# A decoder layer on one core: x loaded a second time, transposed, in place of the first norm's transposes

## The chip, the cores and the metric

The kernel runs on one core of a Trainium2 chip. The metric is the device time of one execution in microseconds (us). An execution uses five engines that run their own instruction queues in order: TensorE (PE in the profile, with its weight loads as PEld), VectorE (DVE), ScalarE (ACT), GpSimd (POOL) and SyncE (SP, which here issues nearly all DMAs). Semaphores order the queues against each other.

## The reference

One layer of a decoder trunk with 256 positions of width 1024, all in float32. Cut to what matters here:

```python
h = rmsnorm(x, ln1_g)                       # x: (256, 1024)
z = h @ w_in                                # 1024 x 2824: pool, mLSTM q/k/v/gates, attention q/k/v
po = pool_mixer(z[pool])                    # windowed means, then 64 x 64 products
hm = mlstm(silu(conv4(z[mq])), silu(conv4(z[mk])), z[v], gates i and f)
ao = attention(rmsnorm(z[aq]), rmsnorm(z[ak]), z[av])
x = x + concat(po, rmsnorm(hm) * sigmoid(z[o]), ao) @ w_out
h2 = rmsnorm(x, ln2_g)
u = conv3(h2 @ w_up)                        # 1024 x 5632
x = x + (silu(u[:2816]) * u[2816:]) @ w_down
```

`rmsnorm(x, g)` is `x * rsqrt(mean(x * x) + eps) * g`. The factor `rsqrt(...)` belongs to a position, the gain `g` to a channel.

## The kernel before

**Products in two parts.** A float32 operand is split into a rounded part "hi" (ACT, `split_hi`, L183) and the rest "lo" (DVE, `split_lo`, L190), and a product is made of three fast matmuls, hi x hi, hi x lo and lo x hi (`product_cols`, `product_rows`, L311 to L322). Where one side is used only once, a plain float32 matmul of the unsplit operands stands in their place (`of_rows`, L446, for the pairs in `FULL`).

**Units.** The weights come in units of 128 partitions by 2048 columns (1 MB), in the order in which PE uses them: unit 0 "of" (output gate and forget gate of the mLSTM, 2080 columns), unit 1 "vi" (values and input gate, 2080), unit 2 pool, 3 mq, 4 mk, 5 akA, 6 aqA and so on, then w_out, w_up and w_down. Four raw buffers (`RAW_BUFS`) hold units as loaded. `load(u)` makes SP issue the load of a unit; `split_lo`, at the last part of unit u, calls `load(u + 4)`, so that load waits in SP's queue until the buffer's readers are done.

**The first norm.** PE needs x with channels on the partitions. x's rows, with the gains beside the first of them, are loaded as `xg` (L216, L217, L220). `first_transpose` (L348) transposes 8 blocks of 128x128 for each half t of the positions, `first_evict` multiplies by the gain on the way out of PSUM (DVE L353, ACT L357), and `first_hi`, `first_lo` (L360, L363) split the result. The norm's factor of a position is not needed for the products: it is put in when they are evicted. `norm_square` (L262) sums the squares of x's rows on ACT, `first_sum` (L371) makes means of them, `guess` (L501, L502) and `newton` (L507 to L509) the factors, and `factors_t` (L385) with `factors` (L389) spread them over the partitions as `rb` for products that have channels on the partitions.

**From the first units on.** ACT evicts of and vi with the factors (`evict_of` L452, L453; `evict_vi` L457, L458). The gate columns of both, for both halves, are transposed by PE (`pg`, L577). From these ACT makes logarithms (`ga`, L582 to L584) and DVE a minimum and two scans (`gm`, `gs`, L589 to L597; L596 copies the running maxima `mr`). The maxima are spread over all partitions by two DMAs that ACT issues: `bm` (L603) writes them to a scratch in DRAM, `br` (L606) reads them back, as soon as `bm` has landed. POOL then masks them (`bs`, L611). DVE evicts pool (`plz`, L781) for a chain of window sums on POOL, and mq and mk (`cz`, L463); ACT scales by the last convolution tap (`cy`, L468), DVE adds the three other taps (`ct`, L476). When all four are done, ACT loads the sigmoid table, makes the sigmoids (`sig`, L485, L488) and loads the old table again (L234). The mLSTM scores (`mS`, L639) follow. akA and aqA are evicted by ACT with squares (`hq`, L515).

**The order of the work** is written out by hand. Every step is a "piece" with a place, a number, from the table `PLACE` or from the default at its `put`. Pieces are emitted in the order of their places, and each engine runs its instructions in that order. PE's products of the bulk, four pieces to a unit, have the whole numbers from 4 on as places: 4 to 7 vi, 8 to 11 pool, 12 to 15 mq, 16 to 19 mk. For example `("hi", 3, 1)`, ACT's split of unit 3's second half, has place 8.84, `bm` 10.076, `br` 10.366, and `("hi", 4, 0)` 9.145.

Before all this PE runs eight matmuls on constants (`keep_warm`, L330), and two more after the first transposes.

Of the kernel before, what the change touches and what calls it, by code (L numbers as in the profile page):

```python
# [9 lines left out]
F32 = mybir.dt.float32  # L10
# [6 lines left out]
P = 128  # L17
# [13 lines left out]
FULL = {(0, q) for q in range(4)} | {(1, 0), (1, 1)}  # L31
# [6 lines left out]
    "n1g": 4.69, "n1n": 4.747, "rbt": 7.327, "rb": 9.568, ("of", 0): 5.309, ("of", 1): 6.265, ("vi", 0): 7.109,  # L38
    ("vi", 1): 7.926, "setup": 5.815, "gain": 16.054, "pg": 7.939, "ga": 8.677, "gm": 9.662, "gs": 9.816,
    "gc": 10.938, "gco": 12.594, "gce": 14.852, ("ply", 0): 41.083, ("plh", 0): 41.762, ("pll", 0): 42,  # L40
    ("ply", 1): 40.544, ("plh", 1): 40.785, ("pll", 1): 41.559, ("plz", 0): 10.494, ("plz", 1): 15.089,
# [54 lines left out]
}  # L96
SPLITS = (4.6, 5.6, 7.6, 9.6, 10.6, 11.6, 12.6, 13.6, 14.6, 16.6)


IN_UNITS = ["of", "vi", "pool", "mq", "mk", "akA", "aqA", "akB", "aqB", "avA", "avB"]  # L100
OUT_K = [0, 2, 4, 6]
N_IN = len(IN_UNITS)
N_OUT = len(OUT_K)
N_DOWN = D_FF // 256
U_OUT = N_IN
U_UP = U_OUT + N_OUT
U_DOWN = U_UP + NPAIR
# [21 lines left out]
def kernel(  # L129
    ctx: ExitStack,  # L130
    tc: tile.TileContext,
    x: bass.AP,
    w: bass.AP,
    wg: bass.AP,
    first: bass.AP,
    params: bass.AP,
    consts: bass.AP,
    out: bass.AP,
):
    nc = tc.nc  # L140

# [43 lines left out]
    def split_lo(u, part, parts):  # L185
# [5 lines left out]
        if part == parts - 1:  # L191
            load(u + RAW_BUFS)
# [1037 lines left out]
```

## Time and profile before

| | us |
|---|---|
| median of 3 runs | 311.16 |
| lowest, highest | 311.11, 312.52 |
| the profiled execution's span | 311.5 |
| PE busy in it | 303.7 (97%) |
| DVE busy | 227.8 (73%) |
| ACT busy | 184.8 (59%) |
| POOL busy | 16.7 (5%) |
| loads and stores of all DMA queues | 54.21 MB, mean 174 GB/s |

The profile is of one execution; its times run from the span's start, which is the first instruction. A row of the instruction views begins with start and duration in us, the engine, the line of the kernel, the operation, and the tiles that it writes and reads ("out<-in"). A bracket tells how long the engine had been idle before and what released it. "SPq" and "ACTq" are those engines' queues of DMA issues. A row of the chain of waits has start, duration and the work on the path that ended last. A row of the waits has the waiting engine and line, whom it waited for, the sum in us, how often, and the longest. In the table of windows each engine's busy time is followed by the granted clock of PE, the DMA engines' busy share and GB/s. The engines' busy shares by themselves decide nothing: PE is busy for 97% of the span, but what it waits for in the remaining time is set by the other queues.

### The profile page before, as it was taken

The page shows a single profiled execution, that of the slowest core. Times are in us where ns is not written, and L with a number is a line of the kernel's source. Part 1 is how long each engine was busy: PE and PEld are TensorE (multiplying, and loading weights), DVE is VectorE, ACT ScalarE, POOL GpSimd, SP SyncE. Part 2 cuts the span into 40 slices and gives each one's busy share as a digit, 9 for nine tenths or more (in the row PEclk, how much of TensorE's full clock was granted, in tenths as well). Part 3 has the DMA queues.
Part 4 walks back from the last instruction along what each step waited for, and adds up shares of the span by engine and source line. Part 5 has one row for each costly group of instructions (what it writes and reads, how often), then busy time and mean ns, then how long its engine had stood idle before and what let it go on. Part 6 is the DMA issues. An engine that isn't in the chain of part 4 may idle for free.

```text
span 311.5 us, 5437 instructions
## 1 busy us (share of the span) xinstructions
PE 303.7 (97%) x2146; PEld 279.0 (90%) x2146; DVE 227.8 (73%) x441; ACT 184.8 (59%) x361; POOL 16.7 (5%) x30
## 2 busy tenths in 40 slices
PE   6999999899999999999999999999999999999995
PEld 3799999899987789999999999999999988888883
DVE  0499899999868657689988788788788786534111
ACT  5398649976888426957575565665664594324000
POOL 1001980000000000000000000000000000000000
PEclk9799999999999999999999999999999999999999
DMA  7985925333704670243564553654544649700003
GB/s 226 424 341 184 347 86 206 128 137 135 263 9 155 252 267 4 97 175 97 185 260 137 179 225 138 203 204 151 214 179 154 239 155 393 276 0 0 0 11 126
DMA packets 8681, 54.21 MB, mean 174 GB/s; under 512 B 964, under 2 KB 1232, under 8 KB 2640
## 3 DMA queue, kind: packets, MB, share of 16 engines
q1 hardware_dynamic: 8352, 52.95, 46.6%
q10 hardware_dynamic: 304, 0.92, 0.9%
q8 instruction: 17, 0.28, 0.3%
q14 instruction: 8, 0.07, 0.1%
HBM read 52.81 MB, written 1.05 MB: 173 GB/s over the span
## 4 chain that ended last, share of the span: by engine, by line
PE 91%; ACT 4%; DVE 3%; issue 1%; DVEq 0%; ACTq 0%
PE dn L824 20%; PE up L313 12%; PE up L311 12%; PE up L312 12%; PE wo L824 7%; PE of L446 2%; DVE mqT L476 2%; PE upr L320 1%; PE upr L322 1%; PE upr L321 1%; PE warm L330 1%; DVE lo L190 1%; PE akB L320 1%; PE n1pt L348 1%; PE pool L311 1%
## 5 line engine op out<-in xcount | busy, mean ns | idle before, releaser
L190 DVE TENSOR_TENSOR lo<-raw,hi 128x1024 fp32r<-128x1024 f32 (+2 forms) x102 | 115.2, 1153 | 18.5 <-ACT hi L183 18.3
L183 ACT ACTIVATE hi<-raw 128x1024 fp32r<-128x1024 f32 (+2 forms) x102 | 98.3, 991 | 28.2 <-PE dn L824 18.6
L311 PE MATMUL up<-h_hi,hi 128*128 128x256 f32 x320 | 90.4, 282 | 0.0
L313 PE MATMUL up<-h_hi,lo 128*128 128x256 f32 x320 | 90.3, 282 | 0.0
L312 PE MATMUL up<-h_lo,hi 128*128 128x256 f32 x320 | 90.3, 282 | 0.0
L313 PEld LDWEIGHTS up<-h_hi,lo 128*128 128x128 f32 x320 | 60.8, 190 | 0.0
L311 PEld LDWEIGHTS up<-h_hi,hi 128*128 128x128 f32 x320 | 60.8, 190 | 0.0
L312 PEld LDWEIGHTS up<-h_lo,hi 128*128 128x128 f32 x320 | 60.8, 190 | 0.0
L1085 DVE SCALAR_TENSOR_TENSOR fy<-up,par,fy 128x255 f32<-128x255 f32 x88 | 41.8, 480 | 15.4 <-ACT fy L1082 13.9
L1082 ACT ACTIVATE fy<-up,par 128x256 f32<-128x256 f32 x44 | 20.1, 466 | 32.4 <-PE up L313 32.4
L824 PE MATMUL dn<-hi,a_hi 128*128 128x512 f32 x88 | 28.1, 392 | 0.0
L824 PE MATMUL dn<-lo,a_hi 128*128 128x512 f32 x88 | 28.1, 392 | 0.0
L824 PE MATMUL dn<-hi,a_lo 128*128 128x512 f32 x88 | 28.1, 392 | 0.0
L824 PEld LDWEIGHTS dn<-hi,a_lo 128*128 128x128 f32 x88 | 16.5, 188 | 3.8
L824 PEld LDWEIGHTS dn<-lo,a_hi 128*128 128x128 f32 x88 | 16.5, 188 | 3.8
L824 PEld LDWEIGHTS dn<-hi,a_hi 128*128 128x128 f32 x88 | 16.5, 188 | 3.7
L238 ACT ACTIVATE a_hi<-fy 128x256 fp32r<-128x256 f32 x22 | 9.2, 418 | 11.8 <-DVE fy L1091 11.8
L1133 DVE TENSOR_TENSOR xg<-dn,xg 128x512 f32<-128x512 f32 (+1 forms) x5 | 2.7, 580 | 16.7 <-PE dn L824 16.7
L824 PE MATMUL wo<-hi,mix_hi 128*128 128x512 f32 x32 | 11.3, 412 | 0.0
L824 PE MATMUL wo<-lo,mix_hi 128*128 128x512 f32 x32 | 10.6, 393 | 0.0
L824 PE MATMUL wo<-hi,mix_lo 128*128 128x512 f32 x32 | 10.6, 393 | 0.0
L1090 ACT ACTIVATE fy<-fy 128x256 f32<-128x256 f32 x22 | 9.0, 408 | 2.2 <-DVE fy L1085 2.2
(287 smaller groups left out, 535.1 us busy)
## 6 DMA issues: line engine op xcount, KB each, us to landing
raw<-in_w SPq DMA_DIRECT2D x46, 1024.0 KB, 4.8
raw<-in_wg SPq DMA_DIRECT2D x2, 520.0 KB, 7.0
raw<-in_wg SPq DMA_DIRECT2D x1, 1040.0 KB
mb<-far ACTq DMA_DIRECT2D x1, 768.0 KB, 7.0
out_y<-xg SPq DMA_DIRECT2D x3, 256.0 KB, 2.1
xg<-in_x SPq DMA_DIRECT2D x1, 512.0 KB, 8.2
par<-in_params SPq DMA_DIRECT2D x1, 337.0 KB, 12.3
xg<-in_first SPq DMA_DIRECT2D x1, 260.0 KB, 2.8
```

What stands on the lines that cost most here:

```text
L183: nc.scalar.activation(hi_t[u][:, s], raw_t[u][:, s], AF.Copy)
L190: nc.vector.tensor_sub(lo_t[u][:, s], raw_t[u][:, s], hi_t[u][:, s].bitcast(F32))
L238: nc.scalar.activation(hi, src, AF.Copy)
L311: nc.tensor.matmul(dst, a, h_hi[:, k, :], start=k == 0, stop=False)
L312: nc.tensor.matmul(dst, a, h_lo[:, k, :], start=False, stop=False)
L313: nc.tensor.matmul(dst, b, h_hi[:, k, :], start=False, stop=k == KT - 1)
L320: nc.tensor.matmul(dst, h_hi[:, k, ts_], hw[:, k, :], start=k == 0, stop=False)
L446: nc.tensor.matmul(ps_t["of", t], h_f[t][:, k, :], w0[:, k, :], start=k == 0, stop=k == KT - 1)
L824: nc.tensor.matmul(acc[t, c], a, b[:, k, o:o + n], start=st and i == 0, stop=sp and i == 2)
L1082: nc.scalar.activation(y, ps[j], AF.Copy, scale=pcol(c0 + 4 * NPAIR))
L1085: nc.vector.scalar_tensor_tensor(y[:, d:], ps[j][:, :S - d], pcol(c0 + 2 * NPAIR * tap), y[:, d:], op0=ALU.mult, op1=ALU.add)
L1090: nc.scalar.activation(y_t[i, 0], y_t[i, 0], AF.Silu)
```

## The change

x is given to the kernel twice: as rows, as before, and transposed (`_xt`: channels on the partitions, the gains in the first 8 columns). The transposed copy, 2056 columns, takes the first raw buffer.

- **Loads.** SP issues, in turn, a quarter of x transposed and a quarter of unit 0, four times; then unit 1's first half, x's rows 0 to 127, unit 1's second half, x's rows 128 to 255; then unit 2, the parameters and the constants. Unit 3 is no longer issued at the start: x transposed holds its buffer, and `split_lo` issues units 3 and 4 together after the last part of unit 0.
- **First norm.** The 16 transposes, their evictions and the two matmuls on constants behind them are gone. For channel blocks of quarters 0 and 1 DVE multiplies by the gain (`first_full`, two instructions of 128x256 a quarter) and PE uses plain float32 products for both halves of the positions; for quarters 2 and 3 `first_hi` and `first_lo` take the gain in themselves, two instructions of 128x256 each, and the product is of three parts. So 8 pairs of channel block and position half are plain products where 12 were.
- **Order.** The first norm's pieces get new places. Both halves of unit 1's rows use its first half of the channels before its second. The sums of squares stand later, just before the guess. Other places that differ:

| piece | before | after |
|---|---|---|
| of, evicted by ACT, t = 0 and 1 | 5.309, 6.265 | 6.2, 6.6 |
| hi of unit 2 | 5.291, 1.571 | 6.4, 6.8 |
| hi of unit 3 | 7.269, 8.84 | 9.95, 10.5 |
| lo of unit 3 | 8.954, 10.243 | 10.1, 10.7 |
| hi of unit 4 | 9.145, 8.886 | 11.75, 12.0 |
| hi of unit 5, first half | 10.09 | 13.6 |
| hi of unit 6, first half | 11.144 | 15.3 |
| lo of units 4 and 5, first halves | 11.57, 13.369 | 11.9, 13.8 |

All others from `rb` (9.568), `bm` and `br` on stay as they were.

```diff
-FULL = {(0, q) for q in range(4)} | {(1, 0), (1, 1)}
+FULL = (0, 1)
...
         if part == parts - 1:
-            load(u + RAW_BUFS)
+            load(u + RAW_BUFS - (u == 0))
+            if u == 0:
+                load(RAW_BUFS)
...
-    nc.sync.dma_start(xg[:, :KT + 512], first[:, :KT + 512])
-    nc.sync.dma_start(xg[:, KT + 512:KT + D], first[:, KT + 512:])
-    load_first(0)
-    load_first(1)
-    nc.sync.dma_start(xs[:, 1], x)
-    load(1)
+    for q in range(4):
+        c = slice(KT * (q > 0) + 2 * S * q, KT + 2 * S * (q + 1))
+        nc.sync.dma_start(x_t[:, c], xt[:, c])
+        load_part(0, q, 4)
+    for t in range(NT):
+        load_part(1, t, 2)
+        nc.sync.dma_start(xs[:, t], x[t * P:(t + 1) * P])
     load(2)
     nc.sync.dma_start(par, params)
-    load(3)
     nc.sync.dma_start(con, consts)
...
+    def first_full(q):
+        for k in (2 * q, 2 * q + 1):
+            nc.vector.tensor_scalar(h_f[:, k, :], xk[:, k, :], g1[:, k:k + 1], None, op0=ALU.mult)
+
+    def first_hi(q):
+        if q in FULL:
+            nc.scalar.activation(h_hi[:, pair(q), :], h_f[:, pair(q), :], AF.Copy)
         else:
+            for k in (2 * q, 2 * q + 1):
+                nc.scalar.activation(h_hi[:, k, :], xk[:, k, :], AF.Copy, scale=g1[:, k:k + 1])
+
+    def first_lo(q):
+        if q in FULL:
+            nc.vector.tensor_sub(h_lo[:, pair(q), :], h_f[:, pair(q), :], h_hi[:, pair(q), :].bitcast(F32))
+        else:
+            for k in (2 * q, 2 * q + 1):
+                nc.vector.scalar_tensor_tensor(h_lo[:, k, :], xk[:, k, :], g1[:, k:k + 1],
+                                               h_hi[:, k, :].bitcast(F32), op0=ALU.mult, op1=ALU.subtract)
...
+    for q in range(4):
+        put(("hi", 1, q), do(split_hi, 1, q, 4), at=(-0.5, 0, 4.4, 4.5)[q])
+        put(("lo", 1, q), do(split_lo, 1, q, 4), ("hi", 1, q), at=(0.5, 1, 4.45, 4.55)[q])
     for t in range(NT):
+        put(("n2", t), do(norm_square, t, 0, 1, "n1", sq1[:, t * D:(t + 1) * D]), at=(4.3, 4.6)[t])
+        put(("sum", t), do(first_sum, t), ("n2", t), at=4.65)
...
-    put("n1g", lambda: guess("n1", n1v[0], [P, NT], "n1"), ("sum", 0), ("sum", 1), at=4.1)
-    put("n1n", do(first_factors), "n1g")
+    put("n1g", lambda: guess("n1", n1v[0], [P, NT], "n1"), ("sum", 0), ("sum", 1), at=4.7)
+    put("n1n", do(first_factors), "n1g", at=4.8)
```

More of the change, by code (lines that the diff above doesn't have):

```diff
@@ L37 @@
 PLACE = {
[L38 to L41, printed above, removed]
[54 rows of a table removed]
+    "rbt": 7.327, "rb": 9.568, ("of", 0): 6.2, ("of", 1): 6.6, ("vi", 0): 7.109, ("vi", 1): 7.926, "setup":
+    5.815, "gain": 16.054, "pg": 7.939, "ga": 8.677, "gm": 9.662, "gs": 9.816, "gc": 10.938, "gco": 12.594, "gce":
+    14.852, ("ply", 0): 41.083, ("plh", 0): 41.762, ("pll", 0): 42, ("ply", 1): 40.544, ("plh", 1): 40.785, ("pll",
[10 rows of a table added]
+    "akA", 1): 23.75, ("hs", "akA", 1): 24.457, ("qe", "aqA", 0): 25.713, ("hq", "aqA", 0): 26.819, ("hs", "aqA",
[11 rows of a table added]
+    "aqB", 0): 34.278, ("qe", "aqB", 1): 35.11, ("hq", "aqB", 1): 37.937, ("hs", "aqB", 1): 37.95, ("hm", "akB"):
[22 rows of a table added]
 }
@@ L134 @@
     wg: bass.AP,
-    first: bass.AP,
+    xt: bass.AP,
     params: bass.AP,
@@ L197, in split @@
             split_lo(u, part, parts)
-    xg = cpool.tile([P, KT + NT * D], F32, name="xg")
-    g1 = xg[:, :KT]
-    xs = xg[:, KT:].rearrange("p (t d) -> p t d", d=D)
+    xs = cpool.tile([P, NT, D], F32, name="xs")
     ident = cpool.tile([P, P], F32, name="ident")
@@ L208, with load_part @@
     nc.gpsimd.affine_select(ident, ones, [[-1, P]], ALU.is_equal, 0.0, base=0, channel_multiplier=1)
+    x_t = wpool.tile([P, UMAX], F32, tag="raw", name="x_t", bufs=RAW_BUFS)
+    g1 = x_t[:, :KT]
+    xk = x_t[:, KT:KT + KT * S].rearrange("p (k c) -> p k c", c=S)
     raw_t[0] = wpool.tile([P, UMAX], F32, tag="raw", name="raw0", bufs=RAW_BUFS)
-    def load_first(c):
-        n = UMAX // 2
-        nc.sync.dma_start(raw_t[0][:, c * n:(c + 1) * n], wg[0][:, c * n:(c + 1) * n])
-    nc.sync.dma_start(xg[:, :KT + 512], first[:, :KT + 512])
-    nc.sync.dma_start(xg[:, KT + 512:KT + D], first[:, KT + 512:])
-    load_first(0)
-    load_first(1)
-    nc.sync.dma_start(xs[:, 1], x)
-    load(1)
+    raw_t[1] = wpool.tile([P, UMAX], F32, tag="raw", name="raw1", bufs=RAW_BUFS)
+    def load_part(u, c, parts):
+        n = UMAX // parts
+        nc.sync.dma_start(raw_t[u][:, c * n:(c + 1) * n], wg[u][:, c * n:(c + 1) * n])
+    for q in range(4):
[5 more added lines that the diff above has]
+        nc.sync.dma_start(xs[:, t], x[t * P:(t + 1) * P])
     load(2)
     nc.sync.dma_start(par, params)
-    load(3)
     nc.sync.dma_start(con, consts)
@@ L337, with pair @@
     table("natural_log_exp_and_others")
-    h_f, r_t, pt1 = {}, {}, {}
+    r_t = {}
     h_fb = wpool.tile([P, UMAX], F32, tag="hi", name="h_f", bufs=HL_BUFS)
+    h_f = h_fb[:, :KT * S].rearrange("p (k c) -> p k c", c=S)
     sq1 = wpool.tile([P, UMAX], F32, tag="lo", name="sq1", bufs=HL_BUFS)
     rb = cpool.tile([P, S], F32, name="rb")
-    HALVES = (slice(0, 4), slice(4, 8))
-    def first_transpose(t):
-        pt1[t] = [aux([P, 4, P], f"n1pt{t}_{b}") for b in range(2)]
-        h_f[t] = h_fb[:, t * D:(t + 1) * D].rearrange("p (k c) -> p k c", c=P)
-        for k in range(KT):
-            nc.tensor.transpose(pt1[t][k // 4][:, k % 4, :], xs[:, t, k * P:(k + 1) * P], ident)
-    def first_evict(t, b, i=0):
-        if (t, b) != (0, 1):
-            ks = HALVES[b]
-            nc.vector.tensor_tensor(h_f[t][:, ks, :], pt1[t][b], g1[:, ks].unsqueeze(2).to_broadcast([P, 4, P]),
-                                    op=ALU.mult)
-        else:
-            for k in range(4 + 2 * i, 6 + 2 * i):
-                nc.scalar.activation(h_f[t][:, k, :], pt1[t][1][:, k - 4, :], AF.Copy, scale=g1[:, k:k + 1])
-    def first_hi(t, b):
-        nc.scalar.activation(h_hi[:, HALVES[b], t * P:(t + 1) * P], h_f[t][:, HALVES[b], :], AF.Copy)
-    def first_lo(t, b):
-        nc.vector.tensor_sub(h_lo[:, HALVES[b], t * P:(t + 1) * P], h_f[t][:, HALVES[b], :],
-                             h_hi[:, HALVES[b], t * P:(t + 1) * P].bitcast(F32))
+    def pair(q):
+        return slice(2 * q, 2 * q + 2)
+    def first_full(q):
[4 more added lines that the diff above has]
+            nc.scalar.activation(h_hi[:, pair(q), :], h_f[:, pair(q), :], AF.Copy)
+        else:
+            for k in (2 * q, 2 * q + 1):
[7 more added lines that the diff above has]
+                                               h_hi[:, k, :].bitcast(F32), op0=ALU.mult, op1=ALU.subtract)
     n1v = []
@@ L442, in of_rows @@
         ks = range(2 * q, 2 * q + 2)
-        if (t, q) in FULL:
+        if q in FULL:
             w0 = operand(raw_t, 0)
             for k in ks:
-                nc.tensor.matmul(ps_t["of", t], h_f[t][:, k, :], w0[:, k, :], start=k == 0, stop=k == KT - 1)
+                nc.tensor.matmul(ps_t["of", t], h_f[:, k, t * P:(t + 1) * P], w0[:, k, :], start=k == 0,
+                                 stop=k == KT - 1)
         else:
@@ L837, in do @@
         return lambda: f(*a)
-    for t in range(NT):
-        put(("T", t), do(first_transpose, t), at=(-9, -8)[t])
-        if t == 0:
-            put(("W", t), do(keep_warm, 2), ("T", t))
-        put(("n2", t), do(norm_square, t, 0, 1, "n1", sq1[:, t * D:(t + 1) * D]), at=(-8.9, 3.8)[t])
-        put(("sum", t), do(first_sum, t), ("n2", t), at=3.9)
-        put(("e", t, 0), do(first_evict, t, 0), ("T", t))
-        for i in range(2 - t):
-            put(("e", t, 1, i), do(first_evict, t, 1, i), ("T", t))
-        for i in range(2):
-            put(("h", t, i), do(first_hi, t, i), *([("e", t, 1, n) for n in range(2 - t)] if i else [("e", t, 0)]))
-            put(("l", t, i), do(first_lo, t, i), ("h", t, i))
@@ L853 @@
-    for u in range(2):
-        for q in range(4):
-            if u == 0 and {(0, q), (1, q)} <= FULL:
-                continue
-            put(("hi", u, q), do(split_hi, u, q, 4), *((("hi", u, q - 1),) if ("hi", u, q - 1) in pieces else ()), at=-7 + 5 * u + q)
-            put(("lo", u, q), do(split_lo, u, q, 4), ("hi", u, q), *((("lo", u, q - 1),) if ("lo", u, q - 1) in pieces else ()))
-    for t in range(NT):
-        for q in range(4):
-            made = [k for k in pieces if k[:3] == ("e", t, q // 2)] if (t, q) in FULL else (("l", t, q // 2), ("lo", 0, q))
-            put(("of", t, q), do(of_rows, t, q), *made, *((("of", t, q - 1),) if q else ()),
-                at=(-4, -2)[t] + q * 0.7)
+    for q in range(4):
+        at = 2 * q - 9
+        if q in FULL:
+            put(("f", q), do(first_full, q), at=at)
+        else:
+            put(("hi", 0, q), do(split_hi, 0, q, 4), at=at + 0.8)
+            put(("lo", 0, q), do(split_lo, 0, q, 4), ("hi", 0, q), at=at + 1.2)
+        put(("h", q), do(first_hi, q), *([("f", q)] if q in FULL else []), at=at + 0.5)
+        put(("l", q), do(first_lo, q), ("h", q), at=at + 1)
+        for t in range(NT):
+            put(("of", t, q), do(of_rows, t, q), *([("f", q)] if q in FULL else [("l", q), ("lo", 0, q)]),
+                *([("of", t, q - 1)] if q else []), at=at + 1.5 + 0.2 * t)
@@ L864 @@
+    for q in range(4):
+        put(("hi", 1, q), do(split_hi, 1, q, 4), at=(-0.5, 0, 4.4, 4.5)[q])
+        put(("lo", 1, q), do(split_lo, 1, q, 4), ("hi", 1, q), at=(0.5, 1, 4.45, 4.55)[q])
+    for t in range(NT):
+        put(("n2", t), do(norm_square, t, 0, 1, "n1", sq1[:, t * D:(t + 1) * D]), at=(4.3, 4.6)[t])
+        put(("sum", t), do(first_sum, t), ("n2", t), at=4.65)
     n = 4
@@ L866 @@
     for name in IN_UNITS[1:]:
-        for j in range(2):
-            for half in range(2):
-                f = bulk_rows if name[:2] in ("vi", "av", "aq", "ak") else bulk_cols
-                put(("b", n), do(f, name, j, half), at=n)
-                done[name, j] = ("b", n)
-                n += 1
+        f = bulk_rows if name[:2] in ("vi", "av", "aq", "ak") else bulk_cols
+        order = [(0, 0), (0, 1), (1, 0), (1, 1)]
+        for j, half in sorted(order, key=lambda o: o[::-1]) if name == "vi" else order:
+            put(("b", n), do(f, name, j, half), at=n)
+            done[name, j] = ("b", n)
+            n += 1
     OUT_ORDER = ((0, 0), (0, 1), (1, 0), (1, 1), (2, 0), (3, 0))
@@ L998 @@
         if n < 8:
-            need(("b", n), ("lo", 1, 1 + 2 * (n % 2)), ("l", n // 6, n % 2))
+            half = n // 6
+            need(("b", n), ("lo", 1, 1 + 2 * half), ("l", 1 + 2 * half))
         elif n < 44:
-            need(("b", n), ("lo", n // 4, n % 2), ("l", 0, 1), ("l", 1, 1))
+            need(("b", n), ("lo", n // 4, n % 2), ("l", 3))
         elif n < 56:
@@ L1196, in _params, with _xt @@
     return p
-def _first(v):
-    return np.ascontiguousarray(np.concatenate([v["ln1_g"][0].reshape(KT, P).T, v["x"][0][:P]], 1))
+def _xt(v):
+    xt = v["x"][0].T.reshape(KT, P, S).transpose(1, 0, 2).reshape(P, KT * S)
+    return np.ascontiguousarray(np.concatenate([v["ln1_g"][0].reshape(KT, P).T, xt], 1))
 def _consts():
@@ L1219 @@
     arrays = {
-        "in_x": np.ascontiguousarray(v["x"][0][P:]), "in_w": w, "in_wg": wg, "in_first": _first(v), "in_params": _params(v),
+        "in_x": v["x"][0], "in_w": w, "in_wg": wg, "in_xt": _xt(v), "in_params": _params(v),
         "in_consts": _consts(),
```

97 rows, old and new, of the table PLACE are left out of this document.

## The prediction

> **What bounds the kernel now.** I read the page, then who TensorE (PE) waited for, then the chain of waits in order of time, then the first 60 us of each queue.
>
> ```profile
> span 311.5 us, 5437 instructions
> ```
> ```profile
> PE of L446 <- DVE h_lo L363: 2.2, 1, 2.2
> ...
> PE akB L320 <- ACT aqAsq L515: 0.8, 1, 0.8
> PE mS L639 <- DVE mkT L492: 0.2, 1, 0.2
> ```
>
> PE is the busy engine, and after the first norm it waits only twice, 1.0 us together: at the first mLSTM scores (mS) and at the first akB product. This looks as if whatever starts PE earlier is gained in full. The chain of waits says what those two waits hang on:
>
> ```profile
> 4.41 1.45 PE n1pt L348 x8
> ...
> 8.49 4.56 PE of L446 x12
> 13.05 0.87 PE n1pt L348 x8
> 13.93 2.63 PE of L446 x12
> ...
> 18.00 0.13 PE vi L320
> ...
> 23.73 0.44 PE n1r L385 x4
> 24.17 0.44 PE pg L577 x4
> ...
> 36.63 0.42 DVE mqz L463
> ...
> 45.46 0.34 DVE mkz L463
> ...
> 46.25 0.46 ACT akAsq L515
> ...
> 56.83 0.39 PE akB L320
> ```
>
> Up to 36.6 us the chain is PE's. Then it is VectorE's (DVE) for nine microseconds, from the second mq eviction to the second mk eviction, then ScalarE's (ACT) through two table loads until akB gets its PSUM buffer at 56.83. PE is not idle meanwhile, but it has only the 0.8 us in hand. So two things must come early for the end to come early: PE's queue, and DVE's arrival at the second mq eviction. If PE comes early and DVE does not, PE simply waits longer at mS and akB.
>
> **The loads.** The change adds a second copy of x, so I count bytes first.
>
> ```profile
> 0.81 0.38 SPq L216 DMA_DIRECT2D xg<-in_first  x1
> ...
> 2.66 0.43 SPq L220 DMA_DIRECT2D xg<-in_x  x1
> ...
> 4.52 1.13 SPq L223 DMA_DIRECT2D par<-in_params  x1
> ```
> ```profile
> xg<-in_x SPq DMA_DIRECT2D x1, 512.0 KB, 8.2
> par<-in_params SPq DMA_DIRECT2D x1, 337.0 KB, 12.3
> xg<-in_first SPq DMA_DIRECT2D x1, 260.0 KB, 2.8
> ```
> ```profile
> 4.00:8.00 4.00, 2.28 (x11) 1.57 (x10) 0.97 (x2) 3.23 (x8) 0.00 (x0) 1.00 0.95 312
> 8.00:12.00 4.00, 3.50 (x9) 2.84 (x10) 1.01 (x2) 1.37 (x3) 0.00 (x0) 0.60 1.02 426
> ```
>
> The last columns of the windows are the DMA engines' share and GB/s: the queue is full from 4 us on. x's second half ends 2068 KB of loads and lands at 2.66 + 8.2 = 10.9 us. The parameters end 4469 KB and land at 4.52 + 12.3 = 16.8. Between them 2401 KB (2.459 MB) took 5.9 us, 0.417 MB/us. In the new order the same 2068 KB are x transposed (1028) and unit 0 (1040): 10.9 again. Then come unit 1's first half, x rows 0, its second half, x rows 1: 2064 KB, 2.114 MB, 5.07 us. So **x's last rows land at 16.0 us instead of 10.9**, unit 2 (1024 KB) at 18.5, parameters and constants at 19.9. Unit 3 now waits for the buffer that x transposed holds; issued near 13 us and queued behind the constants it lands at 22.4, while ACT wants it at 24.7 (below): hidden by 2.3 us.
>
> Bounds for the eight small pieces: if the early stage also ran at 426 GB/s, the four microseconds at 312 would shorten by 4 x (1 - 312/426) = 1.1 us, x's rows at 14.9; at the utmost all 3.966 MB behind the first piece (landed at 0.81 + 2.8 = 3.6) come at 426: 12.9. If the pieces and half units that follow kept to 312, 2.114 MB would take 6.8 us: 17.7. I take 16.0, the row by bytes.
>
> The Trainium skill, "DMA: Bandwidth & Descriptors", section Bandwidth, speaks against this change: batch transfers to 1 MiB or more for 75% of peak. Its fit (section on the anatomy of one DMA, 2.0 us plus bytes over 436 GB/s) makes 2.6 us of a 260 KB piece, as an estimate, and 21 us of eight one after the other. For a single piece the trace agrees, 2.8 us. For a full queue it does not: loads that each take 8 to 12 us from issue to landing were issued one or two microseconds apart and overlap, so the sum goes by bytes.
>
> **PE's early part.** Gone are 16 transposes (1.45 + 0.87 us), two warming matmuls, three DVE evictions and four ACT ones. Added are four DVE scalings of 128x256; the nearest row is
>
> ```profile
> L277 DVE TENSOR_SCALAR n2xn<-xg,rowr 128x512 f32<-128x512 f32 x4 | 1.8, 484 | 0.1
> ```
>
> so at most 0.48 us each, in the shadow of loads that arrive every 0.6 us or slower. The first piece lands at 3.6 us and PE can start near 4.5, not 8.49. It then follows the loads: unit 0's last quarter lands at 10.9, its split takes about 1.1 us (half of the 0.95 and 1.15 found below), and PE ends the first unit near 14.2. Unit 1's products are 2 x 8 x 3 = 48 matmuls at 0.12 us, 5.7 us; its second half lands at 10.9 + 3.8 = 14.7 and is split by 16.4, in time. PE ends unit 1 near 20, against 23.73: **3.7 us earlier, if that were the end of it.**
>
> **What ends last: the gates.** PE goes on to pool only after the gate transposes (pg), and these need of and vi evicted by ACT with the norm's factors, for which both halves of x's rows must have been squared.
>
> ```profile
> 17.49 1.05 ACT L262 ACTIVATE sq<-xg 128x1024 f32<-128x1024 f32 x1
> 18.45 0.18 ACT L262 ACTIVATION_READ_ACCUMULATOR sq<-xg 128x1 f32 x1
> ...
> 20.01 0.20 ACT L501 ACTIVATE n1nt<-n1v 128x2 f32<-128x2 f32 x1 [0.43 <-DVE n1v L371]
> ...
> 21.31 0.24 ACT L452 ACTIVATE gates<-of,n1r 128x4 f32<-128x4 f32 x1
> ...
> 21.81 0.26 ACT L452 ACTIVATE gates<-of,n1r 128x4 f32<-128x4 f32 x1
> ...
> 22.31 0.28 ACT L457 ACTIVATE gates<-vi,n1r 128x4 f32<-128x4 f32 x1
> ...
> 22.82 1.08 ACT L183 ACTIVATE hi<-raw 128x1024 fp32r<-128x1024 f32 x1
> 23.77 0.28 ACT L457 ACTIVATE gates<-vi,n1r 128x4 f32<-128x4 f32 x1
> ```
> ```profile
> 20.88 0.16 DVE L509 SCALAR_TENSOR_TENSOR n1r<-n1nt,n1r 128x2 f32<-128x2 f32 x1
> ```
>
> From 16.0: squares 1.14 (17.49 to 18.63), mean 0.2, guess and Newton 1.03 (20.01 to 21.04): factors at 18.4. Then ACT in its new order: of(0) 0.50, hi of unit 2's first half 0.95, of(1) 0.50, hi of its second half 0.95, vi(0) 0.51, vi(1)'s gates 0.28 and 0.12 to PE: 3.81, pg begins at 22.2 and ends 0.44 later, 22.6; with an estimated 0.05 for each of some eight hand-overs between engines (0.12 from the last gates to pg above), 23.0. Before it ended at 24.61. Unit 2 at 18.5 is in time for its hi at 18.9. So **1.6 us remain of the 3.7**; PE idles some 2 us before pg. An idle 2.2 us before 8.49 was followed by half clock in part of the window 8 to 12 (mean 0.60); if that recurs PE loses up to 1.7 us, and still reaches the end of mq before DVE (next).
>
> **DVE from pg to the second mq eviction** took 36.63 - 24.61 = 12.0 us. In the new order:
>
> ```profile
> 27.98 0.21 DVE L596 COPY mr<-mr 4x128 f32<-4x128 f32 x1
> ...
> 28.46 1.21 DVE L190 TENSOR_TENSOR lo<-raw,hi 128x1024 fp32r<-128x1024 f32 x1
> ...
> 31.14 2.34 DVE L190 TENSOR_TENSOR lo<-raw,hi 128x1024 fp32r<-128x1024 f32 x2
> ...
> 36.63 0.42 DVE L463 TENSOR_TENSOR mqz<-mq,rb 128x256 f32<-128x256 f32 x1 [0.58 <-PE mq L313]
> ```
> ```profile
> 28.23 0.52 ACTq L603 DMA_DIRECT2D far<-mr  x1
> ...
> 29.59 0.39 ACTq L606 DMA_DIRECT2D mb<-far  x1
> ```
>
> - The scans end 3.85 after pg (28.46 - 24.61): 26.9. A lo costs about 1.15.
> - Unit 3's first lo, done before pg until now, comes here: 28.0. Pool's eviction, 0.35: 28.4.
> - Unit 3's second lo needs its hi, and that moves from place 8.84 to 10.5, behind br (10.366), the DMA that ACT issues only when the spread maxima have landed. ACT's instructions go in order, so that hi, unit 4's two, unit 5's and mq's scaling queue behind it. br ended 29.98 - 24.61 = 5.37 after pg: 28.4. The hi ends at 29.4, the lo at 30.6; DVE idles 1.0, and PE's second half of mq waits about 0.2.
> - Unit 4's first lo: 31.8. Unit 5's first hi is fourth behind br: 29.4 + 3 x 0.95 = 32.3; its lo 33.5; unit 4's second 34.6; mq's first and pool's second eviction 35.3.
> - Unit 6's hi, moved from 11.144 to 15.3, now follows mq's scaling: 36.5. Its lo 37.7, gain 0.3: **the second mq eviction at 38.0 instead of 36.63, 1.4 us later.**
>
> PE's mq is done by then even with the half clock. From there to the second mk eviction DVE had no wait, so the delay is carried. GpSimd's pool chain starts about 1.2 us earlier and shares less of that stretch; the pair of lo took 2.89 there
>
> ```profile
> 42.57 2.89 DVE L190 TENSOR_TENSOR lo<-raw,hi 128x1024 fp32r<-128x1024 f32 x2
> ```
>
> against 2.34 at 31.14, so I give back 0.3. **Sum: mS and akB come 1.1 us later.** What follows is PE's queue unchanged: 311.5 + 1.1 in a profiled execution. The median of the runs shown is 311.16, so 312.3 for the median, 0.4% slower: within the half per cent (1.56 us) that a measurement of this kernel can tell.
>
> **Rivals.**
> 1. *Loads early*: x's rows at 14.9 or before. Everything up to the mq eviction moves with them, one for one: 311.2 for 14.9, and 310.2 for 13.9, the middle between that and the utmost. For it: nothing in the DMA queue needs the 312 GB/s stage to recur. Against: it is the same queue, fuller of short rows.
> 2. *PE's early start survives*: br does not hold the hi behind it (no row of before shows it holding one: the next hi was waiting for its own load), so DVE's wait of 1.0 goes, and the 0.6 that it waits for unit 5's hi (31.8 to 32.3 and the hand-over), and loads are at 14.9 or earlier: 1.1 - 1.1 - 1.6 = -1.6, 309.6, and 308.6 for 13.9; I put it at 309.2.
> 3. *Pieces are slow* (the other side of 0.5%): the pieces and halves keep to 312 GB/s, x's rows land at 17.7, pg ends at 24.7, the mq eviction comes 3.1 later: 311.16 + 1.1 + 1.7 = 314.0. It decides from a landing of 16.5 on. The Trainium skill's batching rule above would give this rival; its table's 341 GB/s for a single 1 MB transfer is near that pace.
> 4. *DVE has slack I don't see*, and PE's 1.6 is lost and nothing else: 311.2.
>
> **Chances.** The forecast as summed 0.45 (a quarter of it past 312.7), early loads 0.15, PE's gain surviving 0.13, slow pieces 0.19, unseen slack 0.08. Faster by over 0.5%: 0.13. Slower: 0.19 + 0.11 and a little for pile-ups, 0.32. Within: 0.55. The range takes in early loads and the slow pieces: 309.7 to 314.4; the forecast's own case spans 311.2 to 313.4.
>
> **What would show it.** Right: the first plain matmul of of near 4.5 us; the second square near 16.0; pg ending at 22.5 to 23.5; DVE idle twice, before unit 3's second lo and unit 6's first; the second mq eviction at 37.5 to 38.5; PE's waits at mS and akB growing from 1.0 to about 3.5 us in sum. Wrong: a square before 15 or after 17 (loads), a hi starting while br still waits (ACT's order), or a mq eviction before 36 with PE's waits gone: then the start is gained in full.

## The result and the profile after

| | before | after |
|---|---|---|
| median, us (4 runs each) | 311.13 (310.68 to 312.52) | 314.48 (314.13 to 314.72) |
| ratio, 95% interval | | 1.0113 (1.0083 to 1.0143) |
| span of the profiled execution | 311.5 | 312.4 |

The change makes the kernel 3.35 us slower. The forecast was 312.3 with a range to 314.4. In every execution here the time is the span plus about 1.7 us, so the quoted profile of before, with its span of 311.5, would be a time of some 313.2: it is not an execution near the median. That matters below.

First what PE waits for after the change (the waiting engine and line, whom it waited for, sum, number, longest):

```profile
PE akA L314 <- DVE lo L180: 2.4, 1, 2.4
PE pg L571 <- ACT gates L451: 1.4, 2, 1.1
PE mq L306 <- DVE lo L180: 1.2, 1, 1.2
PE of L439 <- DVE h_f L342: 1.1, 1, 1.1
...
PE akB L313 <- ACT aqAsq L509: 0.8, 1, 0.8
PE mq L304 <- ACT hi L173: 0.7, 1, 0.7
```

Before, only 1.0 us was left after the first norm. Now PE waits in the middle of mq and again at akA, both times for splits. Next ACT's queue after the change, from the second square to the splits behind the broadcast read:

```profile
14.89 1.06 ACT L255 ACTIVATE sq<-xs 128x1024 f32<-128x1024 f32 x1
...
21.45 0.47 ACT L576 ACTIVATE fa<-pg,par 4x256 f32<-4x256 f32 x1
...
25.03 0.52 ACTq L597 DMA_DIRECT2D far<-mr  x1
28.26 0.36 ACTq L600 DMA_DIRECT2D mb<-far  x1
28.67 4.85 ACT L173 ACTIVATE hi<-raw 128x1024 fp32r<-128x1024 f32 x5 [4.63 <-DMA far<-mr]
```

x's rows are squared from 14.89, and the gates' transposes are over before 21.45. So the front of the kernel is early. Then ACT writes the maxima (`far`) and cannot issue the read (`mb`) until 28.26, 3.23 us later, when the write has landed. Five splits wait in its queue for that: ACT is idle for 4.63 us, the first 1.0 of it for the maxima, the rest for the write.

DVE's queue after the change shows who pays:

```profile
26.40 0.41 DVE L775 TENSOR_TENSOR plz<-pool,rb 128x256 f32<-128x256 f32 x1
29.75 2.83 DVE L180 TENSOR_TENSOR lo<-raw,hi 128x1024 fp32r<-128x1024 f32 x2 [2.95 <-ACT hi L173]
...
32.60 3.15 DVE L180 TENSOR_TENSOR lo<-raw,hi 128x1024 fp32r<-128x1024 f32 x2
...
37.68 1.28 DVE L180 TENSOR_TENSOR lo<-raw,hi 128x1024 fp32r<-128x1024 f32 x1 [1.26 <-ACT hi L173]
...
39.37 0.42 DVE L457 TENSOR_TENSOR mqz<-mq,rb 128x256 f32<-128x256 f32 x1
39.70 4.22 DVE L470 SCALAR_TENSOR_TENSOR mqT<-mqz,par,mqT 128x255 f32<-128x255 f32 x6
...
44.17 2.35 DVE L180 TENSOR_TENSOR lo<-raw,hi 128x1024 fp32r<-128x1024 f32 x2
46.44 0.42 DVE L457 TENSOR_TENSOR mkz<-mk,rb 128x256 f32<-128x256 f32 x1
```

Two idle stretches, 2.95 and 1.26 us, and the second mq eviction at 39.37. The chain of waits of after runs through the same places to akB, which stood at 56.83 before:

```profile
25.03 3.21 DMA far<-mr
28.67 1.06 ACT hi L173
29.75 1.71 DVE lo L180
31.48 4.80 DMA raw<-in_w
...
37.68 1.28 DVE lo L180
...
58.01 0.39 PE akB L313
```

Between the two low parts the profile leads the chain through a load that landed at 36.28. Whether that load or the place of unit 6's split makes the second idle is tried below.

### The profile page after: what moved, and what is told of

The parts are those of the page before. It is cut to its first block, busy times and chain, and to the rows that moved or that the text cites. A ratio compares the mean times of both kernels' runs of the same rounds, so it can differ in the third digit from the quotient of the medians.

```text
span 312.4 us, 5418 instructions
## 1 busy us (share of the span) xinstructions
PE 299.7 (96%) x2132; PEld 274.4 (88%) x2132; DVE 227.3 (73%) x444; ACT 184.7 (59%) x359; POOL 11.9 (4%) x30
## 4 chain that ended last, share of the span: by engine, by line
PE 80%; DMA 7%; ACT 6%; DVE 5%; issue 1%; SPq 0%; ACTq 0%; DVEq 0%
PE dn L818 19%; PE up L306 12%; PE up L304 12%; PE up L305 12%; PE wo L818 7%; DMA xs<-in_x 2%; ACT hi L173 2%; DVE lo L180 2%; DMA raw<-in_wg 2%; DMA raw<-in_w 2%; PE upr L313 1%; DVE mqT L470 1%; PE upr L315 1%; PE upr L314 1%; DMA far<-mr 1%; PE akB L313 1%
## 5 line engine op out<-in xcount | busy, mean ns | idle before, releaser
L1123 DVE TENSOR_TENSOR xs<-dn,xs 128x512 f32<-128x512 f32 (+1 forms) x5 | 2.7, 579 | 16.7 <-PE dn L818 16.7
```

## The experiments

Each time stands beside runs of the kernel before on the same chip. What is said below of the executions of the kernel before rests on those runs and the ones of the unchanged copy, 92 together. Where a diff shows only added numbers, they are added at the end of the table `PLACE`.

**The kernel before, unchanged**, for another profile of it.

> The kernel before, unchanged, to see how its span and its measured time hang together. Theory (the profiled execution of before was not a typical one): a run's time is its span plus about 1.7 us, as in the kernel after (314.13 for a span of 312.4), so a median of 311.1 means a typical span near 309.4, and 311.5 was an execution with PE's clock halved between 8.8 and 12.3 us. Rival (before carries less around its span): spans of 311 to 312 at times of 311.1.

Measured: 310.83 us, ratio 1.0002 (0.9975 to 1.0030). This execution has a span of 309.0. Its marks on PE, ACT and DVE, one fence for each view:

```profile
7.72 2.87 PE L446 MATMUL of<-raw,h_f 128*128 128x260 f32 x12 [1.08 <-DMA raw<-in_wg]
```
```profile
22.17 0.47 ACT L582 ACTIVATE fa<-pg,par 4x256 f32<-4x256 f32 x1 [0.22 <-PE pg L577]
...
25.75 0.52 ACTq L603 DMA_DIRECT2D far<-mr  x1
...
27.11 0.39 ACTq L606 DMA_DIRECT2D mb<-far  x1
```
```profile
34.16 0.42 DVE L463 TENSOR_TENSOR mqz<-mq,rb 128x256 f32<-128x256 f32 x1 [0.58 <-PE mq L313]
34.50 5.34 DVE L476 SCALAR_TENSOR_TENSOR mqT<-mqz,par,mqT 128x255 f32<-128x255 f32 x6
...
40.10 2.89 DVE L190 TENSOR_TENSOR lo<-raw,hi 128x1024 fp32r<-128x1024 f32 x2
42.91 0.41 DVE L463 TENSOR_TENSOR mkz<-mk,rb 128x256 f32<-128x256 f32 x1
```

The first twelve products start at 7.72 and take 2.87 us here. In the quoted profile they started at 8.49 and took 4.56, and from their end on everything stands 2.5 us earlier here (34.16 against 36.63, 42.91 against 45.39). The distances are the same: from the gates' start on ACT to the second mq eviction 12.0 us in both. So of the 2.5 us, 0.8 was lost ahead of the products (PE had waited 2.22 us there and 1.08 here) and 1.7 in them. The windows of the quoted profile show the 1.7 (second column: PE's busy time; then, third from the end, the granted clock):

```profile
5.42:8.84 3.42, 1.20 (x8) 0.70 (x7) 1.70 (x3) 2.46 (x8) 0.00 (x0) 1.00 0.94 341
8.84:12.25 3.41, 3.41 (x10) 2.65 (x9) 0.17 (x1) 1.16 (x2) 0.00 (x0) 0.50 1.01 424
```

For 3.41 us PE had half clock. Of the 92 runs, 13 lie between 312.51 and 313.06 at a mean clock of 0.995, and 79 between 309.89 and 311.52 at 0.997 or more. The quoted profile, at 0.995, is one of the 13's kind. Why its products also started 0.8 us later, and whether those of the 13 did, the record does not show.

**The new places alone**: the kernel before, with only the splits of units 3 to 6 where the change puts them.

```diff
+    **{("hi", 3, 0): 9.95, ("hi", 3, 1): 10.5, ("hi", 4, 0): 11.75, ("hi", 4, 1): 12.0, ("hi", 5, 0): 13.6,
+       ("hi", 6, 0): 15.3, ("lo", 3, 0): 10.1, ("lo", 3, 1): 10.7, ("lo", 4, 0): 11.9, ("lo", 5, 0): 13.8},
```

> The kernel before with only the new places of the splits of units 3 to 6, none of the loads or of the first norm changed. Theory: br holds unit 3's second hi here too, the second mq eviction comes 1.5 to 2 us later and the time rises to about 312.8. Rival (the places matter only with the new loads): 311.1.

Measured: 314.15 us, ratio 1.0094 (1.0063 to 1.0124). On DVE:

```profile
28.64 2.84 DVE L191 TENSOR_TENSOR lo<-raw,hi 128x1024 fp32r<-128x1024 f32 x2 [1.09 <-ACT hi L184]
...
36.77 1.56 DVE L191 TENSOR_TENSOR lo<-raw,hi 128x1024 fp32r<-128x1024 f32 x1 [1.26 <-ACT hi L184]
...
38.74 0.41 DVE L464 TENSOR_TENSOR mqz<-mq,rb 128x256 f32<-128x256 f32 x1
```

Ten numbers in a table, with no load and no norm touched, make the kernel 3.4 us slower (314.15 against 310.74 beside it): as much as the whole change, and 1.35 more than expected. The two idles are those that the prediction named, at 1.09 and 1.26 nearly with its sizes, since in this kernel the write lands in 1.36 us (25.78 to 27.14). The second mq eviction is 2.1 us later than in the quoted profile, near what was expected, but 4.6 later than in the unchanged copy: the expectation was made against the same unusual execution as the prediction. Of the 4.6, the idles are 2.35 and unit 3's first low part, which now stands behind the gates, 1.2; the other low parts took some 1.7 longer, and 0.9 that DVE had waited for PE is gone. The delay reaches PE at akA:

```profile
PE akA L322 <- DVE lo L191: 3.0, 1, 3.0
```

This profile, at 314.54 and a mean clock of 0.994, has half clock from 46.3 to 49.7, right behind that wait. The three executions at full clock took 313.86 to 314.15, so the half clock is the smaller part of the loss.

**The changed kernel with units 3 and 4 split ahead of the write and the read.**

```diff
+    **{("hi", 3, 1): 10.02, ("hi", 4, 0): 10.04, ("hi", 4, 1): 10.06},
```

> The kernel after, with ACT's hi of unit 3's second half and of unit 4 put ahead of bm and br again (places 10.02, 10.04, 10.06). Theory (DVE's arrival at the second mq eviction sets the end, and br holds the hi behind it): DVE's wait of 2.95 us before unit 3's second lo goes, the second mq eviction comes at about 36 instead of 39.4, and the time falls by about 2.5 us to 312.0, since GpSimd then shares more of the taps. Rival (loads decide, or PE's own queue): the time stays within 0.5 us of 314.5.

Measured: 313.12 us, ratio 1.0073 (1.0048 to 1.0098). The idle before unit 3's second low part is gone; one of 1.03 us now stands before unit 4's second low part and unit 5's first, and that of 1.26 is left. The second mq eviction starts at 36.42, 2.95 earlier than in the changed kernel, but the median gains only 1.4, not the 2.5 expected. Eight of its ten executions have a clock of 0.988 to 0.995 and times of 312.74 to 314.74; the two at full clock took 311.86 and 311.88. So the lower clock comes with about 1.3 us of the median; where it falls, the one profile, at full clock, does not show.

**All splits ahead**: those of units 5 and 6 as well, unit 6's just before ACT's mq scaling.

```diff
+    **{("hi", 3, 1): 10.02, ("hi", 4, 0): 10.04, ("hi", 4, 1): 10.06, ("hi", 5, 0): 10.09, ("hi", 6, 0): 14.3},
```

> As the kernel with the hi ahead, and unit 5's first hi between bm and br and unit 6's first hi ahead of mq's scaling (10.09 and 14.3). Theory: DVE's second wait, 1.26 us before unit 6's first lo, goes too; 0.8 to 1.0 us less than with the first three alone, 311.1. Rival (unit 6 lands too late for it): the same time as that one, or more.

Measured: 309.66 us, ratio 0.9958 (0.9937 to 0.9979). It beats both kernels. It is 3.5 below the median with the first three splits alone, and 2.1 below in the profiled executions at full clock (307.9 against 310.0 of span), where 0.8 to 1.0 was expected. On ACT and on DVE:

```profile
24.96 0.51 ACTq L598 DMA_DIRECT2D far<-mr  x1
25.90 1.04 ACT L174 ACTIVATE hi<-raw 128x1024 fp32r<-128x1024 f32 x1
27.43 1.06 ACT L174 ACTIVATE hi<-raw 128x1024 fp32r<-128x1024 f32 x1 [0.49 <-DMA raw<-in_w]
29.00 0.36 ACTq L601 DMA_DIRECT2D mb<-far  x1
```
```profile
31.94 1.20 DVE L181 TENSOR_TENSOR lo<-raw,hi 128x1024 fp32r<-128x1024 f32 x1
33.07 0.57 DVE L418 SCALAR_TENSOR_TENSOR gg<-par 128x1 f32<-128x1 f32 x1
33.57 0.41 DVE L458 TENSOR_TENSOR mqz<-mq,rb 128x256 f32<-128x256 f32 x1
```

The write now takes 4.04 us to land, the longest of all, and nobody minds: splits run meanwhile, and DVE waits for no high part. With its splits ahead, then, the changed kernel is 1.1 us faster than the kernel before. How much of that the new loads and the new first norm bring by themselves is not shown, since the kernel before was not run with these same places.

**The read moved instead of the splits.** In the changed kernel all splits keep their new places; `br` and `bs` go behind unit 5's second split.

```diff
+    **{"br": 14.25, "bs": 14.3},
```

> The changed kernel with its two broadcast reads of the mask moved behind unit 5's second split (places 14.25 and 14.3); every split keeps its new place. Theory (the read, which waits for another transfer, holds the splits queued behind it on ACT): VectorE's idle of 2.95 us behind two missing high parts goes, that of 1.26 us before unit 6's low part stays, the scaling that follows the second mq eviction starts at about 36 instead of 39.37, and the median is about 311 (310 to 312.5). Rival (the places themselves cost it, whatever stands ahead of them): the scaling starts after 38.5 and the median stays at 314.5.

Measured: 312.05 us (310.27 to 312.97), ratio 1.0030 (1.0008 to 1.0052). On DVE:

```profile
26.41 2.76 DVE L181 TENSOR_TENSOR lo<-raw,hi 128x1024 fp32r<-128x1024 f32 x2
...
33.99 1.22 DVE L181 TENSOR_TENSOR lo<-raw,hi 128x1024 fp32r<-128x1024 f32 x1 [1.26 <-ACT hi L174]
...
35.20 0.42 DVE L458 TENSOR_TENSOR mqz<-mq,rb 128x256 f32<-128x256 f32 x1
```

The idle of 2.95 is gone, that of 1.26 is there, the second mq eviction starts at 35.20: the read held the splits. The executions spread over 2.7 us, five of ten at a clock of 0.991 to 0.994.

**The same, with unit 6's split ahead of the mq scaling.**

```diff
+    **{"br": 14.25, "bs": 14.3, ("hi", 6, 0): 14.26},
```

> The same, and unit 6's split too at 14.26, ahead of ACT's mq scaling. Theory: the idle of 1.26 us before unit 6's low part goes as well, the scaling starts at 33.5 to 35, the median is about 309.5 (309 to 310.5), as where all the splits were moved ahead. Rival (unit 6's place costs nothing, since the gates' end decides): no more than 0.3 us under the kernel with the reads alone moved.

Measured: 310.58 us, ratio 0.9965 (0.9942 to 0.9988). The second idle is gone too, with nothing but the place of unit 6's split changed, and so are the executions at less than 0.997; the second mq eviction starts at 34.45. The median is 0.1 us outside what was expected, and 0.9 above the kernel with all splits ahead.

**Both**: all splits ahead, the read late.

```diff
+    **{("hi", 3, 1): 10.02, ("hi", 4, 0): 10.04, ("hi", 4, 1): 10.06, ("hi", 5, 0): 10.09, ("hi", 6, 0): 14.26,
+       "br": 14.25, "bs": 14.3},
```

> All the splits ahead of the broadcast reads, and the reads late as well. Theory (once no split stands behind the reads they hold nothing that matters): the same as the kernel with all splits ahead, 309.66, within 0.5 us. Rival (the reads still hold the gates' work on ACT behind them for a part of their 4.0 us): 308.7 or less.

Measured: 309.65 us, ratio 0.9959 (0.9941 to 0.9978), the same as without the late read. Once no split stands behind the read, it holds nothing that counts.

**One more load.** The kernel before, and the kernel with the new places alone, each with a load of 960 KB behind the first ones, which nothing reads.

```diff
     nc.sync.dma_start(con, consts)
+    spare = cpool.tile([P, 1920], F32, name="spare")
+    nc.sync.dma_start(spare, w[2][:, :1920])
```

> The kernel before with one more load of 960 KB, which nothing reads, behind its first loads (about as many bytes as the second copy of x adds). Theory (the small write of the maxima lands late because it shares the DMA engines with the bulk of the loads): the write is followed by its read back after 3 us or more instead of 1.36; the splits stand ahead of the read in this kernel, so the second mq scaling moves by less than 1 us and the median stays at 310.7 to 311.7. Rival (the late landing has another cause in the changed kernel): it stays at 1.4.

> The kernel before with the new places of the splits alone and the same unused load. Theory (with the splits behind the read, its late landing goes straight to the end): the read back comes 3 us or more after the write, the second mq scaling starts at 40 to 41 instead of 38.74, and the median is 315 to 316.5 instead of 314.15. Rival (the landing does not matter to the end): 314.15 within 0.5.

Measured: 310.88 us for the first, ratio 1.0005 (0.9995 to 1.0016); 314.86 for the second, ratio 1.0148 (1.0120 to 1.0176). ACT's queue in the first and in the second:

```profile
25.32 0.52 ACTq L605 DMA_DIRECT2D far<-mr  x1
...
28.64 0.36 ACTq L608 DMA_DIRECT2D mb<-far  x1
```
```profile
25.55 0.51 ACTq L606 DMA_DIRECT2D far<-mr  x1
29.02 0.36 ACTq L609 DMA_DIRECT2D mb<-far  x1
29.43 4.86 ACT L184 ACTIVATE hi<-raw 128x1024 fp32r<-128x1024 f32 x5 [4.88 <-DMA far<-mr]
```

With 960 KB more ahead of it the write of 6 KB takes 3.32 and 3.47 us instead of 1.36. With the splits ahead of the read that costs nothing. With the splits behind it DVE idles 3.20 us instead of 1.09 and the second mq eviction starts at 39.90 instead of 38.74. Both numbers of the second kernel fall 0.1 us short of what was expected. Of the 1.16 us by which the mq eviction moves, 0.7 reaches the median. All four executions with the load are at a clock of 0.993 or 0.994, though, and against the two such executions of the places alone (314.51, 314.54) the load costs only 0.3.

**PE's gap ahead of the first products.** The kernel before, with nine, five and no matmuls on constants behind the first transposes instead of two.

```diff
-            put(("W", t), do(keep_warm, 2), ("T", t))
+            put(("W", t), do(keep_warm, 9), ("T", t))
```

> The kernel before with 9 instead of 2 idle matmuls behind the first transposes, which fill PE's gap ahead of the first norm's work. Theory (the executions at a mean clock of 0.995 and some 313 us are those in which PE's gap there brought half clock): median 310.7 as before, and none or nearly none of its executions above 312, where the kernel before has 5 of 36. Rival (half clock comes elsewhere, or whatever PE does there): the share above 312 stays at about one in seven.

> The kernel before with five instead of two such matmuls. Theory: none of its executions at a clock of 0.995 and some 313 us, median 310.8 within 0.5. Rival: one in seven of them.

> The kernel before without the two matmuls on constants behind the first transposes, so that PE does still less ahead of the product of unit 0. Theory (too little work there brings half clock in some executions): executions at a clock of 0.995 and some 313 us become more frequent than the 10 of 67 of the kernel before, half of them or more. Rival (that work decides nothing): they stay at about one in seven.

Measured: 311.29 us with nine, 310.96 with five, 311.47 with none (310.20 to 314.40). Executions at a clock of 0.995 or less: none of ten, none of ten, five of ten, where the kernel before has 13 of 92. (One run with nine reached 312.43, at full clock.) At 13 in 92, twenty executions without one would come about 1 time in 20, (79/92)^20 = 0.05. So half clock came more often with less of PE's work in that gap and not at all with more, though chance is not quite ruled out; no version with more of it improved the median.

## Why the prediction was wrong, point by point

**The step that failed** is the last of the sum: "What follows is PE's queue unchanged: 311.5 + 1.1 in a profiled execution. The median of the runs shown is 311.16, so 312.3 for the median". The profiled execution was taken to stand for the median. It lay 2.5 us of span above the usual 309.0: 1.7 by the half clock whose row (0.60 in the window from 8 to 12) the prediction itself quoted and used only as a risk of after, and 0.8 by a later start of the first products. Against 311.5 the sum is right to 0.2 us: akB starts 1.18 later (56.83 to 58.01), the span is 0.9 longer. Against a usual execution of before the same end point lies 2.5 us further away: the profile of after has neither the late start nor that half clock (PE starts on the products at 5.21), and its own waits are what sets the end. 0.9 + 2.5 = 3.4 is the loss measured. The sum's own end, a span of 312.6, set against 309.0 would have been a loss of 3.6. (Two of after's four executions have a mean clock of 0.993 and 0.994 too; their spans, 312.6 and 312.9, lie between those of the other two.)

What the sum should have held against a usual execution, by DVE's marks of the unchanged kernel and of after:

| | before, usual | after | difference |
|---|---|---|---|
| gates start on ACT | 22.17 | 21.45 | -0.7 |
| from there to the second mq eviction | 11.99 | 17.92 | +5.9 |
| from there to the second mk eviction | 8.75 | 7.07 | -1.7 |
| sum | 42.91 | 46.44 | +3.5 |

The 5.9 is made up of 4.2 of idle for the two splits, 1.2 for unit 3's first low part, which now stands behind the gates, and 1.2 by which the other low parts were slower, less 0.9 that DVE no longer waits for PE; 0.2 is in small instructions.

**Its terms**, each against the trace:

- *Loads.* x's last rows: 16.0 forecast, 14.89 measured, the "loads early" bound of 14.9. The windows of after (GB/s in the last column) show 356 and 424, where before had 312 and 426:

```profile
4.00:8.00 4.00, 2.90 (x13) 2.18 (x13) 2.12 (x6) 1.45 (x3) 0.00 (x0) 1.00 0.97 356
8.00:12.00 4.00, 3.55 (x23) 2.86 (x22) 3.59 (x8) 3.50 (x8) 0.00 (x0) 1.00 1.04 424
```

  So small pieces did not slow the queue, and the rival of slow pieces, whose number came nearest (314.0), had the wrong mechanism. The rival of early loads had the landing right and the time wrong (311.2), since it stood on the same base. The rival by which the read holds no split is refuted by the runs that moved it.
- *PE's start.* 4.5 forecast, 5.21 measured; the first piece landed at 4.49, not 3.6. Nothing hung on it.
- *Gates.* 23.0 forecast, 21.45 at the latest measured; 1.1 of the difference comes from the loads. Against the quoted profile (24.61) that would be a gain of 3.2, against a usual before it is 0.7.
- *The read holds the splits.* Right, and shown by moving either side. Its price was taken from before's landing of 1.36; after needed 3.23. DVE idled 2.95 instead of the 1.0 forecast.
- *Unit 6's split behind the mq scaling.* Forecast about 1.2 of idle, measured 1.26.
- *Low parts.* Two pairs of them took 2.83 and 3.15 us instead of 2.34 each (1.3 more). This was not in the sum. GpSimd's pool chain ran beside a part of them (28.82 to 30.38, 32.09 to 33.54), and with all splits ahead the pairs took 2.34 while the chain's first window sum took 4.94 us, against 0.61 in the changed kernel, where DVE idled. So the two engines seem to slow each other, which was not tried by itself.
- *Second mq eviction.* 38.0 forecast, 39.37 measured: 1.55 early at the gates, 2.9 more behind them.
- *What is given back.* 0.3 forecast; the taps took 4.22 instead of 5.34 and the pair of low parts 2.35 instead of 2.89, together 1.7. That error of 1.4 and the one before, 1.4 the other way, cancel, which is why akB came out at 1.18 with 1.1 forecast. The agreement is partly luck.
- *PE's waits.* Forecast at mS and akB, some 3.5 us; they came earlier, at mq (1.9) and akA (2.4), and akB kept 0.8.

**The causes in order**, by medians: the new places, 3.4; the late landing behind more loads, 0.7 in the kernel before with both; what the early loads and norm give back then, 0.4 (314.86 to 314.48), against 1.1 where the splits are ahead. These three steps add to 3.7, the change's own pair of medians gives 3.35; the medians of the kernel before itself differ by as much (311.13, 310.74, 310.90, 310.80). The first step is clear (ratio 1.0063 to 1.0124). The other two are smaller than the 0.9 us or so that such an interval leaves to either side, and 0.4 of the 0.7 may be the clock, so their sizes are rough; that the late landing lengthens DVE's idle, from 1.09 to 3.20, is shown.

What stays open: in which place the executions with late splits lose their clock (0.988 to 0.995 in eight of ten with units 3 and 4 ahead, in five of ten with the late read). Two profiles of other kernels with late splits were at such a clock, and in both half clock follows PE's waits, in different places: with the new places alone from 46.3 to 49.7, behind the wait of 3.0 at akA; with the load besides from 32.9 to 36.3, behind waits of 0.9 and 1.0 in mq. In the profile with units 3 and 4 ahead PE waits 2.8 us at akA and yet keeps full clock, so such a wait does not bring it each time. Nor is the one execution with all splits ahead explained that had a mean clock of 0.951 and yet took only 310.82.

## What to carry to other kernels

Before a sum is made against a profiled execution, its span is compared with the median and its clock row is read: an execution that has lost 2 us for a reason that the change removes or never had is no base. Where ACT issued a transfer that must wait for another, everything behind it in ACT's queue waited for the landing as well, so work that others need goes ahead of the issue; then the landing's length did not matter here (4.04 us without an idle of DVE with the splits ahead, 3.23 us with one of 2.95 in the changed kernel). A change that brings both a new mechanism and new places for old work is best judged with each alone: here the places alone cost 3.4 us, and the change with its splits ahead gained 1.1.

## What the runs showed of the hardware

A write of 6 KB, with its read issued on the landing, took 1.36 us with the DMA engines at a share of 0.45 of the window from 24 to 28 us, and 3.23 to 4.04 where that window's share was 0.82 or more:

```profile
24.00:28.00 4.00, 4.00 (x35) 3.85 (x34) 3.90 (x8) 3.59 (x5) 0.32 (x1) 1.00 0.45 186
```
```profile
24.00:28.00 4.00, 4.00 (x36) 3.85 (x35) 2.73 (x6) 0.03 (x1) 0.96 (x3) 1.00 0.91 376
```

(The first is the unchanged kernel, the second the changed one.) The Trainium skill, "DMA: Bandwidth & Descriptors", section "Latency and other measured facts", has an access to HBM at 0.2 us on average and 2 us at high load; the difference measured here, 1.9 to 2.7 us, is of that size or somewhat more. That the added load makes the write late is shown (1.36 to 3.32 and 3.47); whether in the memory or in the DMA engines is not.

In the quoted profile the clock went to half for 3.41 us after a stretch of 3.42 us in which PE had still worked for 1.20 us; the kernel before shows such a mean clock in about one execution in seven. In the two profiles with late splits at a lower clock, half clock lasted 3.4 us as well, after stretches of that length in which PE had worked for about 1.5 us. In the unchanged copy PE worked for 2.34 us in the stretch ahead of 8.84, and the clock stayed full. The Trainium skill, "TensorE: Matmul & The Clock Gate", Part 1, has a free-running window of 3.4 us, which agrees, and puts half clock after at least one idle window; here the stretches ahead were not idle. How much work keeps the clock up is not settled by these runs.
